# Rotary queries of a four-branch decoder kernel: turned with channels on partitions, stacked by way of DRAM

## The chip, the core and the metric

The kernel runs on one core of one Trainium2 chip. A core has TensorE (matrix products, PE in the profile, with its weight loads as PEld), VectorE (DVE), ScalarE (ACT), GpSimd (POOL) and SyncE (SP, which here issues every DMA). Matrix products land in PSUM, everything else works in SBUF, and large tensors lie in DRAM. The metric is the device time of one execution in microseconds (us), the median of several runs.

## The reference, cut to what matters

Two layers of a decoder trunk over 1024 tokens of width 1024. Each layer projects the stream, mixes the tokens in four ways (latent attention "MLA" with a rotary part, stick-breaking attention, forgetting attention "fox", attention to a memory), gates and projects each branch, merges them, and normalizes. The change touches only the rotary part of the MLA queries (four heads of 64 plain and 32 rotary channels):

```python
q = (_rms_norm(c_q, q_norm) @ w_qb).reshape(b, s, MLA_HEADS, MLA_NOPE + MLA_ROPE)
q_nope, q_pe = q[..., :MLA_NOPE], q[..., MLA_NOPE:]
q_pe = _rope(q_pe, cos[:, :, None, :], sin[:, :, None, :])
...
y_mla = _causal_softmax_attention(jnp.concatenate([q_nope, q_pe], -1),
                                  jnp.concatenate([k_nope, k_pe], -1), v_mla)
```

where `_rope` splits the 32 channels into halves x1, x2 and returns `[x1*cos - x2*sin, x1*sin + x2*cos]`. The angles depend on the token alone, so all heads and both layers share one table of 16 cosines and one of 16 sines for each token. The queries are scaled by 96 to the power -1/2.

## The kernel before, in words

**Arithmetic.** Every fp32 product is made of three fast products: an operand a is split into a high part (a rounded to the fast format fp32r) and a low part (what is left), and a.b is ah.bh + ah.bl + al.bh. `passes` (L242) emits these three matmuls for each 128-row block of the contraction (lines 245, 246, 247 of the profile). A split costs one copy and one subtraction. For the score products, the two parts of a head's 64 channels are stacked on 128 partitions (`stack_pair`, L286: ACT writes the high parts at L291, DVE the low parts at L295), so that one matmul contracts both.

**Buffers.** Most tiles of 128 x 512 words come from one pool "U" of 64 buffers; seven larger "W" buffers hold 128 x 1024. PSUM has eight banks: two of tag "pt" (`PT`), four of "pj" (`PJ`), two of "y". A tile that finds no free buffer waits for one to be released.

**Order.** The program is written as generators. A main one emits its instructions, and at each of its `yield`s a side one may emit a few of its own, so that TensorE has other work while a result is split. A scheduler then orders each engine's instructions once, at build time; on the chip each engine takes its own list in that order and waits at semaphores. DMAs are all in SP's list, so a DMA that has to wait holds those behind it.

**One layer.** Latent keys and values are projected and stored (`ckv_d`), then the fox branch runs in two pairs of heads: `run(units, filler, total)` emits the score and value products of the units and spreads `total` steps of a filler, here the projections of the next pair, over their gaps. The stick-breaking branch, the memory branch and the gates follow. Then comes the MLA preparation, which the change is about. Its main generator is, in order: `mla_ckvT` (latents with channels on partitions, rotary key), `mla_k`, `load_wq` (the query weights, split on POOL by `split_pool`, L153), `load_cq(1)`, `mla_v`, `split_cq(1)` (normalized query latents of tokens 512 to 1023, "half 1"), `load_cq(0)`, `mla_qpe(1)`, `split_cq(0)`, `mla_q(1)`, `mla_qpe(0)`, `mla_qpT(1)`, `mla_q(0)`, `mla_qpT(0)`. Beside it runs `early()`: the last gates, then 26 steps of the merge of a finished branch (products "pg" and "pb", accumulated by DVE into "acc" tiles). Each of the first 19 yields of the main generator, every fourth from the 20th, and some extra ones (a `yield n` stands for n steps) bring one such step; what is left is emitted when the main generator ends. The MLA units follow, heads 0 to 3, and in each head the query blocks in the order 3, 0, 2, 1 (256 tokens each): the first unit needs half 1, the second half 0.

**The rotary queries.** `mla_qpe(half)` (L990) projects the 4 x 32 rotary channels of 512 tokens with channels on partitions (nine matmuls into "qpeT"), copies them to SBUF on ACT (L994), yields three side steps, transposes the four 128 x 128 blocks back to tokens on partitions (L998), turns them there with six DVE operations of 128 x 256 (L703 to L708), scales them on POOL (L1004), and writes four tiles in which each head's 32 channels stand as high, low, high, low (four ACT copies at L1010, four DVE subtractions at L1011). `mla_qpT(half)` (L1015) transposes these for each head, four 128 x 128 blocks each (L1019), and ACT copies the result out of PSUM (L1021). The tile "qpe" of a head and half then holds 128 rows: the 32 channels as high, low, high, low. The score matmul at L369 contracts it with the rotary key.

Of the kernel before, what the change touches and what calls it, by code (L numbers as in the profile page):

```python
# [10 lines left out]
F32 = mybir.dt.float32  # L11
F32R = mybir.dt.float32r
I32 = mybir.dt.int32
AF = mybir.ActivationFunctionType
ALU = mybir.AluOpType
# [12 lines left out]
MG_FROM = 20  # L28
MG_EVERY = 4
CQ_STEPS = 1  # L30
QPE_STEPS = 3
MG_LATE = 16
Q_ORDER = (3, 0, 2, 1)
NB = S // P
# [31 lines left out]
def decoder_trunk(ctx: ExitStack, tc: tile.TileContext, x, x_t, mem_t, positions, w_a, w_s, mla_q_norm, mla_w_qb,  # L66
# [31 lines left out]
    def TMP(s="tmp"):  # L98
        return tp.tile([P, HALF], F32, tag="tmp", name=nm(s))
# [13 lines left out]
    def f(ap):  # L113
        return ap.bitcast(F32)
# [38 lines left out]
    def split_pool(src, h, l):  # L153
        i = pool.tensor_scalar(h, src, 1.0, 1.0, ALU.mult, ALU.mult)  # L154
        if hold[0] is not None:
            after(i, hold[0])
        pool.tensor_tensor(l, src, f(h), ALU.subtract)  # L157
# [27 lines left out]
    y_d = dp.tile([2 * KVR, S], F32, name="y_d")  # L185
    gt_d = dp.tile([KVR, S], F32, name="gt_d")
    c_d = dp.tile([4, S], F32, name="c_d")

    def rsqrt(dst, m, n):
        t = SM("rs_t", n)  # L190
# [138 lines left out]
    def pair_qkv(op, scale):  # L329
        op["q"], op["k"] = two_halves(), two_halves()  # L330
        yield from proj(stack_pair(op["q"], scale))
        yield from proj(stack_pair(op["k"], 1.0))
        vT = [None, None]

        def evac(ps, half):
            vT[half] = U("vT", F32)
            act.copy(vT[half], ps)
        yield from proj(evac)
        op["v"] = v_from_T(vT, NB)
        yield  # L340
# [149 lines left out]
    def chain(*gens):  # L490
        for g in gens:
            yield from g
# [30 lines left out]
    def run(units, filler, total, rest=True):  # L523


        order = list(units)
        gaps = sum(len(u.chunks()) * 2 + (1 if u.kind == "mem" else 2 + 2 * (u.qg // 2)) for u in units)
        done = [0, 0]

        def gap():  # L530
            done[0] += 1
            want = done[0] * total // gaps
            steps(filler, want - done[1])
            done[1] = want
# [12 lines left out]
        if rest:  # L547
            drain(filler)
# [60 lines left out]
    def angles():  # L609
# [7 lines left out]
        for dst, shift in ((sinT, 0.0), (cosT, 0.25)):  # L617
# [9 lines left out]
            dve.tensor_scalar(dst, dst, 3.1415925, -3.1415925, ALU.min, ALU.max)  # L627
            tfn(dst, dst, AF.Sin)

    for layer in range(DEPTH):  # L630
        last_layer = layer == DEPTH - 1
        xsrc = x[0] if layer == 0 else xs
# [68 lines left out]
        def rope(dst, src, cs, sn, t, mul):  # L701
            x1, x2 = src[..., 0:16], src[..., 16:32]
            mul(dst[..., 0:16], x1, cs, ALU.mult)  # L703
            mul(t, x2, sn, ALU.mult)
            mul(dst[..., 0:16], dst[..., 0:16], t, ALU.subtract)
            mul(dst[..., 16:32], x1, sn, ALU.mult)
            mul(t, x2, cs, ALU.mult)
            mul(dst[..., 16:32], dst[..., 16:32], t, ALU.add)  # L708
# [134 lines left out]
        drain(pair_qkv(fox[0], SC64))  # L843
        fox[0].update(new_op())
        ys[(2, 0)] = fox[0]["y"]
        run(fox_units(fox[0], 0), pair_qkv(fox[1], SC64), 49)
        fox[1].update(new_op())
        ys[(2, 1)] = fox[1]["y"]
        run(fox_units(fox[1], 1), pair_qkv(sb[0], SC64), 49)
# [93 lines left out]

        qpe = [[None, None] for _ in range(4)]
        cqT = [[], []]
        t4s = [[], []]
        cq_raw = [[], []]

        def load_cq(half):
# [21 lines left out]
        def load_wq():  # L971
            for k in range(3):
                raw = rp.tile([P, HALF], F32, tag="wr", name=nm("wr"))
                nc.sync.dma_start(raw[:, :384], mla_w_qb[layer, k * P:(k + 1) * P, :])
                h, l = U("wqh"), U("wql")
                sv = raw[:, :384].rearrange("p (h c) -> p h c", h=4)
                for c0, c1, d0 in ((0, 64, 0), (64, 96, 256)):
                    n = 4 * (c1 - c0)
                    hv, lv = (t[:, d0:d0 + n].rearrange("p (h c) -> p h c", h=4) for t in (h, l))
                    split_pool(sv[:, :, c0:c1], hv, lv)  # L980
                wq_h.append(h)
                wq_l.append(l)

        def mla_q(half):
            for pair in range(2):
                ps = PJ()
                yield from passes(ps, wsl(wq_h, wq_l, 3, pair * P), cqT[half], 3)
                stack_pair(ml[pair]["q"], SC96, True)(ps, half)

        def mla_qpe(half):  # L990
            ps = PJ("qpeT")
            yield from passes(ps, wsl(wq_h, wq_l, 3, 256), cqT[half], 3)
            qT = U("qT", F32)
            act.copy(qT, ps)  # L994
            yield QPE_STEPS
            ps = PT("qpe")
            for b in range(4):
                pe.transpose(ps[:, b * P:(b + 1) * P], qT[:, b * P:(b + 1) * P], ident)  # L998
            src = ps.rearrange("p (b h c) -> p b h c", b=4, h=4)
            qr = U("qr", F32).rearrange("p (b h c) -> p b h c", b=4, h=4)  # L1000
            qt = TMP("qt")[:, :256].rearrange("p (b h c) -> p b h c", b=4, h=4)
            cs, sn = (t[:, 4 * half:4 * half + 4].unsqueeze(2).broadcast_to((P, 4, 4, 16)) for t in (cosT, sinT))
            rope(qr, src, cs, sn, qt, dve.tensor_tensor)
            pool.tensor_scalar(qr, qr, SC96, 1.0, ALU.mult, ALU.mult)  # L1004
            for b2 in range(2):
                t4 = wp.tile([P, 2, 4, 4, ROPE], F32R, tag="W", name=nm("qt4"))
                for b in range(2):
                    t = t4[:, b]
                    qb_ = qr[:, 2 * b2 + b].unsqueeze(2).broadcast_to((P, 4, 2, ROPE))
                    act.copy(t[:, :, 0::2, :], qb_)  # L1010
                    dve.tensor_tensor(t[:, :, 1::2, :], qb_, f(t[:, :, 0::2, :]), ALU.subtract)  # L1011
                    t4s[half].append(t)
            yield

        def mla_qpT(half):  # L1015
            for h in range(4):
                pt = PT("qpT")
                for b in range(4):
                    pe.transpose(pt[:, b * P:(b + 1) * P].bitcast(F32R), t4s[half][b][:, h].rearrange("p a c -> p (a c)"), ident_r)  # L1019
                o = U("qpe")  # L1020
                act.copy(o, pt)  # L1021
                qpe[h][half] = o
                yield
            t4s[half].clear()


        yb = {}
# [79 lines left out]
        def step(f):  # L1107
            f()
            yield

        main = chain(mla_ckvT(), mla_k(0), mla_k(1), step(load_wq), step(lambda: load_cq(1)), mla_v(0), mla_v(1),
                     split_cq(1), step(lambda: load_cq(0)), mla_qpe(1), split_cq(0), mla_q(1), mla_qpe(0), mla_qpT(1), mla_q(0), mla_qpT(0))

        def early():
            for _ in side:
# [177 lines left out]
```

## Time and profile before

| | |
|---|---|
| median of 3 runs | 1590.06 us (1589.10 to 1591.06) |
| the profiled execution | 1590.93 us, span 1589.2 us from its first to its last instruction |
| mean granted TensorE clock in it | 0.995 |
| MLA preparation, layer 0 | about 470 to 528 us of the span |
| the same, layer 1 | about 1262 to 1320 us |

The profile shows one execution. Its page gives each engine's busy time, the chain of work that ended last, and groups of instructions by source line with count, total and mean time. Other views of the trace list the instructions of a stretch in order of time, the waits by who waited for whom, or the busy time of each engine in chosen stretches. In the list by time a row has start, duration (of a group, the time that it covers), engine, line, operation, output and inputs, count, and in brackets the idle time before it with what ended it. Matmuls overlap, so a matmul's duration is longer than its share of TensorE: that share is the distance from its start to the next one's.

### The profile page before, as it was taken

What the parts mean: (1) busy time and instruction counts of PE and PEld (TensorE: products, weight loads), DVE (VectorE), ACT (ScalarE), POOL (GpSimd) and SP (SyncE); (2) the same over time, 40 slices, a digit from 0 to 9 for tenths busy, and PEclk for the clock granted to TensorE, in tenths of its full rate; (3) what the DMA queues carried; (4) which work ended last, traced back from release to release, by engine and by line L of the source; (5) the groups of instructions that cost most, each with busy time, mean ns of one, the idle gap of its engine ahead of it and who ended that gap; (6) DMA issues with size and microseconds to landing.
All of it is one profiled execution on the core that took longest, in us unless ns stands there. A gap on an engine that the chain in (4) does not pass through costs nothing.

```text
span 1589.2 us, 24849 instructions
## 1 busy us (share of the span) xinstructions
PE 1559.1 (98%) x8454; PEld 1332.1 (84%) x8454; DVE 1035.0 (65%) x2025; ACT 739.9 (47%) x1632; POOL 834.8 (53%) x991
## 2 busy tenths in 40 slices
PE   9999999999999999999999999999999999999997
PEld 8888888888888888888788888888888878888885
DVE  7456689844436788872763566898444367888638
ACT  4355656534424656440423556555344346564302
POOL 5676435765544344671836655267655433446515
PEclk9999999999999999999999999999999999999999
DMA  6311112142233211252312221122422332212413
GB/s 183 114 57 55 48 39 64 54 127 61 79 102 110 68 58 40 82 177 73 116 61 87 60 61 44 37 64 64 116 61 84 100 104 70 64 49 75 146 53 113
DMA packets 86062, 127.93 MB, mean 80 GB/s; under 512 B 13424, under 2 KB 38832, under 8 KB 85936
## 3 DMA queue, kind: packets, MB, share of 16 engines
q1 hardware_dynamic: 85936, 126.34, 25.6%
q8 instruction: 67, 1.10, 0.3%
q14 instruction: 59, 0.48, 0.1%
HBM read 89.57 MB, written 19.96 MB: 69 GB/s over the span
## 4 chain that ended last, share of the span: by engine, by line
PE 85%; DVE 7%; issue 2%; DMA 2%; POOL 2%; ACT 1%; SPq 0%; DVEq 0%; ACTq 0%; POOLq 0%
PE pj L245 12%; PE pj L246 12%; PE pj L247 12%; PE y L485 7%; PE pt L455 6%; PE sc L366 3%; PE sc L367 3%; PE pb L245 3%; PE po L245 3%; PE po L247 3%; PE po L246 3%; PE pb L247 3%; PE pb L246 3%; PE pg L245 2%; PE pg L247 1%
## 5 line engine op out<-in xcount | busy, mean ns | idle before, releaser
L245 PE MATMUL pj<-xTh,wh 128*128 128x512 f32 x832 | 331.6, 399 | 2.2 <-DVE mx L424 1.4
L247 PE MATMUL pj<-xTh,wl 128*128 128x512 f32 x832 | 326.5, 392 | 0.0
L246 PE MATMUL pj<-xTl,wh 128*128 128x512 f32 x832 | 326.0, 392 | 0.0
L157 POOL TENSOR_TENSOR wl<-wr,wh 128x512 fp32r<-128x512 f32 x168 | 229.9, 1370 | 9.8
L154 POOL TENSOR_SCALAR wh<-wr 128x512 fp32r<-128x512 f32 x168 | 116.3, 692 | 209.7 <-PE pj L246 112.9
L146 DVE TENSOR_TENSOR pl<-pt,ph 128x384 fp32r<-128x384 f32 (+1 forms) x272 | 170.4, 638 | 75.3 <-ACT ph L145 73.4
L145 ACT CAST ph<-pt 128x384 fp32r<-128x384 f32 (+1 forms) x272 | 147.0, 550 | 133.9 <-PE pt L455 127.6
L247 PEld LDWEIGHTS pj<-xTh,wl 128*128 128x128 f32 x832 | 156.4, 188 | 31.8
L245 PEld LDWEIGHTS pj<-xTh,wh 128*128 128x128 f32 x832 | 156.8, 188 | 28.8 <-DVE mx L424 1.8
L246 PEld LDWEIGHTS pj<-xTl,wh 128*128 128x128 f32 x832 | 156.8, 189 | 25.4
L436 POOL TENSOR_SCALAR p<-p,sm 128x896 f32<-128x896 f32 (+7 forms) x128 | 102.4, 801 | 144.0 <-DVE sm L435 142.4
L125 ACT ACTIVATE p<-p,mx 128x896 f32<-128x896 f32 (+7 forms) x128 | 99.5, 778 | 70.7 <-DVE mx L424 63.2
L485 PE MATMUL y<-pl,v 128*128 128x256 f32 (+1 forms) x544 | 125.5, 307 | 0.0
L125 ACT ACTIVATE mg<-pg 128x512 f32<-128x512 f32 x128 | 76.4, 597 | 88.0 <-PE pg L247 58.9
L485 PE MATMUL y<-ph,v 128*128 128x256 f32 (+1 forms) x544 | 112.6, 284 | 0.1
L455 PE MATMUL pt<-ident_r,p 128*128 128x128 f32 x704 | 110.5, 272 | 0.0
L245 PE MATMUL pb<-ybh,wh 128*128 128x512 f32 x256 | 102.9, 402 | 2.2 <-DVE opB L295 1.0
L485 PEld LDWEIGHTS y<-ph,v 128*128 128x128 f32 x544 | 93.7, 190 | 12.3 <-issue 0.9
L429 DVE TENSOR_TENSOR_SCAN kt<-kt,unseen 128x896 f32<-128x896 f32 (+3 forms) x64 | 94.5, 1489 | 10.1 <-ACT kt L125 9.8
L246 PE MATMUL pb<-ybl,wh 128*128 128x512 f32 x256 | 100.1, 391 | 0.0
L247 PE MATMUL pb<-ybh,wl 128*128 128x512 f32 x256 | 100.1, 391 | 0.0
L416 POOL TENSOR_SCALAR_AFFINE_SELECT bt<-bt 128x128 f32<-128x128 f32 x64 | 47.5, 745 | 95.0 <-ACT bt L125 91.2
(277 smaller groups left out, 3658.0 us busy)
## 6 DMA issues: line engine op xcount, KB each, us to landing
wr<-in_w_s_dram SPq DMA_DIRECT2D x168, 256.0 KB, 2.6
s<-opA SPq DMA_DIRECT2D x128, 64.0 KB, 2.0
s<-opB SPq DMA_DIRECT2D x128, 64.0 KB, 2.0
wr<-in_w_out_dram SPq DMA_DIRECT2D x32, 256.0 KB, 2.6
xr<-in_x_t_dram SPq DMA_DIRECT2D x16, 256.0 KB, 5.1
ckb<-c_d SPq DMA_DIRECT2D x8, 512.0 KB, 3.8
y_d<-y SPq DMA_DIRECT2D x16, 256.0 KB, 2.0
y<-y_d SPq DMA_DIRECT2D x16, 256.0 KB, 3.6
```

The costliest lines, as they stand in the source:

```text
L125: i = act.activation(*args, **kw)
L145: act.copy(h, src)
L146: return dve.tensor_tensor(l, src, f(h), ALU.subtract)
L154: i = pool.tensor_scalar(h, src, 1.0, 1.0, ALU.mult, ALU.mult)
L157: pool.tensor_tensor(l, src, f(h), ALU.subtract)
L245: pe.matmul(ps, ah, bh, start=k == 0, stop=False)
L246: pe.matmul(ps, ah, bl, start=False, stop=False)
L247: pe.matmul(ps, al, bh, start=False, stop=k == nk - 1)
L429: dve.tensor_tensor_scan(kt[:, ::-1], kt[:, ::-1], unseen[:, S - w:][:, ::-1], 1.0, ALU.mult, ALU.max)
L436: pool.tensor_scalar(p, p, sm, 1.0, ALU.mult, ALU.mult)
L455: pe.transpose(pt[:, c:c + P], self.p[i][:, b * P:(b + 1) * P], ident)
L485: pe.matmul(u.y[:, q0 * P:256], u.op["v"][b][:, u.head, :], src[:, s * 256 + q0 * P:s * 256 + 256], start=j == 0 and n == 0, stop=j == n_c ...
```

## The change

The rotary part of the queries is turned where the projection leaves it, with channels on partitions and tokens along the row, and is brought to its stacked form by DMA.

- The rotary columns of the query weight are put down as first halves of all heads, then second halves (`load_wq`), so that rows 0 to 63 of the projection are the x1 and rows 64 to 127 the x2 of the four heads.
- Tables with channels on partitions are made once, in layer 0, as four extra steps of the filler of the first fox run (whose total goes from 49 to 53): for cosine and sine and each half, POOL spreads the table (tile "rows"), TensorE transposes four 128 x 128 blocks, ACT scales them (for the sine in two pieces, the second with a minus sign), and a DMA stores 256 KB to `tab_d`.
- `mla_qpe` reads the projection straight from PSUM, which is now a "pt" bank. Four DVE operations turn it, ACT rounds the high part, POOL subtracts for the low part, two DMAs store both to `qr_d`, and eight DMAs (two for each head) load 64 rows each: x1 and x2 of high and low, the same rows twice.
- `mla_qpT`, the transpositions in `mla_qpe`, the copies around them and the three side steps are gone. The main generator loads the tables beside the latents, and `mla_qpe(0)` now stands ahead of `mla_q(1)`.

```diff
@@ new, in layer 0 only
+    def rotary_tables():
+        for n, src in enumerate((cosT, sinT)):
+            for half in range(2):
+                rows = U("rows", F32)
+                pool.tensor_scalar(rows.rearrange("p (b r c) -> p b r c", b=4, r=8),
+                                   src[:, 4 * half:4 * half + 4, :].unsqueeze(2).broadcast_to((P, 4, 8, 16)), 1.0, 1.0, ALU.mult, ALU.mult)
+                ps = PT("tab")
+                for b in range(4):
+                    pe.transpose(ps[:, b * P:(b + 1) * P], rows[:, b * P:(b + 1) * P], ident)
+                t = TMP("tab")
+                if n == 0:
+                    act.activation(t, ps, AF.Copy, scale=SC96)
+                else:
+                    act.activation(t[0:64, :], ps[0:64, :], AF.Copy, scale=SC96)
+                    act.activation(t[64:128, :], ps[64:128, :], AF.Copy, scale=-SC96)
+                nc.sync.dma_start(tab_d[2 * half + n], t)
+                yield
@@
-        run(fox_units(fox[0], 0), pair_qkv(fox[1], SC64), 49)
+        tables = () if layer else rotary_tables()
+        run(fox_units(fox[0], 0), chain(pair_qkv(fox[1], SC64), tables), 49 if layer else 53)
@@ mla_qpe
-            ps = PJ("qpeT")
+            ps = PT("qpeT")
             yield from passes(ps, wsl(wq_h, wq_l, 3, 256), cqT[half], 3)
-            qT = U("qT", F32)
-            act.copy(qT, ps)
-            yield QPE_STEPS
-            ps = PT("qpe")
-            for b in range(4):
-                pe.transpose(ps[:, b * P:(b + 1) * P], qT[:, b * P:(b + 1) * P], ident)
...
-            rope(qr, src, cs, sn, qt, dve.tensor_tensor)
-            pool.tensor_scalar(qr, qr, SC96, 1.0, ALU.mult, ALU.mult)
-            for b2 in range(2):
...
-                    act.copy(t[:, :, 0::2, :], qb_)
-                    dve.tensor_tensor(t[:, :, 1::2, :], qb_, f(t[:, :, 0::2, :]), ALU.subtract)
+            cs, sn = tabs.pop(half)
+            r = U("qr", F32)
+            t = U("qt", F32)
+            dve.tensor_tensor(t[0:64, :], ps[64:128, :], sn[64:128, :], ALU.mult)
+            dve.tensor_tensor(t[64:128, :], ps[0:64, :], sn[0:64, :], ALU.mult)
+            dve.tensor_tensor(r, ps, cs, ALU.mult)
+            dve.tensor_tensor(r, r, t, ALU.add)
+            h, l = U("qrh"), U("qrl")
+            act.copy(h, r)
+            nc.sync.dma_start(f(qr_d[2 * half]), f(h))
+            pool.tensor_tensor(l, r, f(h), ALU.subtract)
+            nc.sync.dma_start(f(qr_d[2 * half + 1]), f(l))
             yield
+            src = f(qr_d[2 * half:2 * half + 2]).rearrange("a (t h c) n -> h (a t) c n", t=2, h=4)
+            for hd in range(4):
                 o = U("qpe")
+                for n in range(2):
+                    nc.sync.dma_start(f(o[64 * n:64 * n + 64, :]), src[hd])
+                qpe[hd][half] = o
+            yield
@@ mla_qpT, removed
-            for h in range(4):
-                pt = PT("qpT")
-                for b in range(4):
-                    pe.transpose(pt[:, b * P:(b + 1) * P].bitcast(F32R), t4s[half][b][:, h].rearrange("p a c -> p (a c)"), ident_r)
-                o = U("qpe")
-                act.copy(o, pt)
@@ the main generator
-        main = chain(mla_ckvT(), mla_k(0), mla_k(1), step(load_wq), step(lambda: load_cq(1)), mla_v(0), mla_v(1),
-                     split_cq(1), step(lambda: load_cq(0)), mla_qpe(1), split_cq(0), mla_q(1), mla_qpe(0), mla_qpT(1), mla_q(0), mla_qpT(0))
+        main = chain(mla_ckvT(), mla_k(0), mla_k(1), step(load_wq), step(lambda: load_cq(1)), step(lambda: load_tabs(1)), mla_v(0), mla_v(1),
+                     split_cq(1), step(lambda: load_cq(0)), step(lambda: load_tabs(0)), mla_qpe(1), split_cq(0), mla_qpe(0), mla_q(1), mla_q(0))
```

`load_tabs(half)` takes two U buffers and issues two loads of 256 KB from `tab_d`.

More of the change, by code (lines that the diff above doesn't have):

```diff
@@ L30 @@
 CQ_STEPS = 1
-QPE_STEPS = 3
 MG_LATE = 16
@@ L187, in decoder_trunk @@
     c_d = dp.tile([4, S], F32, name="c_d")
+    tab_d = dp.tile([4, P, HALF], F32, name="tab_d")
+    qr_d = dp.tile([4, P, HALF], F32R, name="qr_d")
     def rsqrt(dst, m, n):
@@ L945, in decoder_trunk @@
         cqT = [[], []]
-        t4s = [[], []]
         cq_raw = [[], []]
@@ L976, in load_wq @@
                 sv = raw[:, :384].rearrange("p (h c) -> p h c", h=4)
[L977 to L980, printed above, removed]
+                hv, lv = (t[:, :256].rearrange("p (h c) -> p h c", h=4) for t in (h, l))
+                split_pool(sv[:, :, 0:64], hv, lv)
+                hv, lv = (t[:, 256:384].rearrange("p (t h c) -> p t h c", t=2, h=4) for t in (h, l))
+                split_pool(sv[:, :, 64:96].rearrange("p h (t c) -> p t h c", t=2), hv, lv)
                 wq_h.append(h)
@@ L988, in mla_q, with load_tabs @@
                 stack_pair(ml[pair]["q"], SC96, True)(ps, half)
+        tabs = {}
+        def load_tabs(half):
+            tabs[half] = [U("tab", F32), U("tab", F32)]
+            for n, t in enumerate(tabs[half]):
+                nc.sync.dma_start(t, tab_d[2 * half + n])
         def mla_qpe(half):
-            ps = PJ("qpeT")
+            ps = PT("qpeT")
             yield from passes(ps, wsl(wq_h, wq_l, 3, 256), cqT[half], 3)
-            qT = U("qT", F32)
-            act.copy(qT, ps)
-            yield QPE_STEPS
@@ L996, in mla_qpe @@
-            ps = PT("qpe")
-            for b in range(4):
[L998 to L1002, printed above, removed]
-            rope(qr, src, cs, sn, qt, dve.tensor_tensor)
@@ L1004, in mla_qpe @@
-            pool.tensor_scalar(qr, qr, SC96, 1.0, ALU.mult, ALU.mult)
-            for b2 in range(2):
[L1006 to L1009, printed above, removed]
-                    act.copy(t[:, :, 0::2, :], qb_)
-                    dve.tensor_tensor(t[:, :, 1::2, :], qb_, f(t[:, :, 0::2, :]), ALU.subtract)
-                    t4s[half].append(t)
@@ L1013, in mla_qpe @@
-            yield
-        def mla_qpT(half):
-            for h in range(4):
-                pt = PT("qpT")
-                for b in range(4):
-                    pe.transpose(pt[:, b * P:(b + 1) * P].bitcast(F32R), t4s[half][b][:, h].rearrange("p a c -> p (a c)"), ident_r)
+            cs, sn = tabs.pop(half)
[3 more added lines that the diff above has]
+            dve.tensor_tensor(t[64:128, :], ps[0:64, :], sn[0:64, :], ALU.mult)
@@ L1022, in mla_qpT @@
-                qpe[h][half] = o
-                yield
-            t4s[half].clear()
+                for n in range(2):
+                    nc.sync.dma_start(f(o[64 * n:64 * n + 64, :]), src[hd])
+                qpe[hd][half] = o
+            yield
         yb = {}
```

## The prediction

> **What bounds the kernel now.** I read the page's first part first, then its chain.
>
> ```profile
> span 1589.2 us, 24849 instructions
> PE 1559.1 (98%) x8454; PEld 1332.1 (84%) x8454; DVE 1035.0 (65%) x2025; ACT 739.9 (47%) x1632; POOL 834.8 (53%) x991
> PE 85%; DVE 7%; issue 2%; DMA 2%; POOL 2%; ACT 1%; SPq 0%; DVEq 0%; ACTq 0%; POOLq 0%
> ```
>
> TensorE is busy for 98% of the span and is 85% of the chain that ended last. An average says nothing about one stage, so next the busy time by stretch, for the stretches that the change touches: the fox run of layer 0 that gets the tables, and the MLA preparation of both layers. The columns are PE, PEld, DVE, ACT, POOL, clock, DMA share and GB/s.
>
> ```profile
> 110.00:140.00 30.00, 30.00 (x170) 25.81 (x169) 14.97 (x48) 14.49 (x34) 16.54 (x25) 1.00 0.16 49
> 470.00:504.00 34.00, 32.59 (x170) 26.95 (x169) 18.14 (x31) 16.31 (x32) 15.72 (x22) 1.00 0.36 116
> 504.00:535.00 31.00, 30.21 (x157) 24.30 (x156) 22.67 (x47) 17.75 (x36) 5.05 (x6) 1.00 0.11 31
> 1296.00:1327.00 31.00, 30.22 (x157) 24.30 (x156) 23.07 (x47) 18.08 (x36) 5.05 (x6) 1.00 0.12 33
> ```
>
> TensorE is without a gap where the tables come in, and idle for 0.79 of 31 us where the transpositions go out. Both layers run the latter stretch alike, so one is worked out and doubled. The clock is full, and DMA has room. A transposition taken out of such a stretch is worth the TensorE time that it occupies.
>
> **Removed from TensorE.** The list by time, layer 0:
>
> ```profile
> 504.63 0.60 PE L998 MATMUL qpe<-ident_r,qT 128*128 128x128 f32 x4
> 505.07 0.60 PE L959 MATMUL rqb<-ident_r,rq 128*128 128x128 f32 x4
> 512.69 0.39 PE L245 MATMUL qpeT<-cqh,wqh 128*128 128x512 f32 x1
> 512.92 0.39 PE L246 MATMUL qpeT<-cql,wqh 128*128 128x512 f32 x1
> 524.76 0.46 PE L1019 MATMUL qpT<-ident_r,qt 128*128 128x128 f32 x4
> 525.06 0.47 PE L246 MATMUL pj<-cql,wqh 128*128 128x512 f32 x1
> 525.37 0.46 PE L1019 MATMUL qpT<-ident_r,qt 128*128 128x128 f32 x4
> 531.86 0.40 PE L247 MATMUL pg<-mrh,wl 128*128 128x512 f32 x1
> 532.81 0.36 PE L1019 MATMUL qpT<-ident_r,qt 128*128 128x128 f32 x2 [0.56 <-ACT qpe L1021]
> ```
>
> From start to start a 512-column matmul takes 512.92 - 512.69 = 0.23. A group of four L1019 transpositions takes 525.06 - 524.76 = 0.30, and the matmul behind it 525.37 - 525.06 = 0.31 in place of 0.23, so 0.38 for a group; eight groups a layer (two halves, four heads) make 3.0 us. A group at L998 takes 505.07 - 504.63 = 0.44; two make 0.9. Last, 531.86 + 0.23 = 532.09, and the next matmul starts at 532.81: 0.7 us in which PE waits for the ACT copy of an earlier transposed head. That wait goes with L1021; what is late next there is nothing that I see, since only score and merge products follow. Together 4.6 us a layer, 9.2 for both.
>
> Here the Trainium skill reads otherwise: "TensorE: Matmul & The Clock Gate", Part 4, gives about 275 ns for a 128x128 transposition in a kernel. By it, 80 removed and 16 added make 64 x 0.275 = 17.6 us, an estimate of mine from that figure. It is the duration of a single one; four of them start within 0.30 to 0.44 above, so I do not use it in the sum.
>
> **Added to TensorE.** Sixteen transpositions for the tables, once. The nearest row is the same operation in the same fox run:
>
> ```profile
> 122.36 0.60 PE L319 MATMUL vtp<-ident_r,vT 128*128 128x128 f32 x4
> 122.72 0.48 PE L366 MATMUL sc<-opA,opA 128*128 128x512 f32 x1
> 123.04 0.39 PE L367 MATMUL sc<-opA,s 128*128 128x512 f32 x1
> ```
>
> 0.36 for the group, and 0.32 in place of 0.23 behind it: 0.45, four times 1.8 us. No idle time covers it. ACT and POOL have half of that stretch free for the spreading and scaling, and the four stores end hundreds of microseconds before the first load.
>
> **Other engines.** In a half, ten DVE operations of 256 columns, nine ACT copies of 256 or 512 columns and a POOL scaling become four DVE operations, one ACT copy and one POOL subtraction. All of it lies beside TensorE (DVE is busy for 22.67 of 31 us there), so I cost the saving at nothing, and it can only help. The weight split keeps four POOL instructions a block with the same sizes: nothing. The three side steps that each `mla_qpe` gave away are not lost: by my count of yields, 42 side steps are all emitted inside the main generator before, 36 after, and the other six between `mla_q(0)` and the first scores. That moves work, and costs none. `mla_qpe(0)` stands directly behind `split_cq(0)`, whose splits it needs; `mla_q(1)`, emitted after it, is ready earlier, and the scheduler can put its 18 matmuls (4.1 us) into that gap.
>
> **The new round trip.** The rows for its steps: two DVE operations, the rounding copy, the POOL subtraction, DMA issue on SP, and DMA time to landing of a 256 KB store and load and a 64 KB move; then when the inputs are there and when the result is wanted.
>
> ```profile
> L961 DVE TENSOR_TENSOR cq<-cq,rqb x12: 677/681/687, 484.9 to 1299.1; 128x512 f32<-128x512 f32 x12
> L295 DVE SCALAR_TENSOR_TENSOR opB<-pj,opB x56: 692/694/694, 41.9 to 1325.7; 64x512 fp32r<-64x512 f32 x56
> L1021 ACT CAST qpe<-qpT x16: 585/588/618, 519.9 to 1326.7; 128x512 fp32r<-128x512 f32 x16
> L157 POOL TENSOR_TENSOR wl<-wr,wh x168: 1272/1292/2868, 21.7 to 1477.0; 128x512 fp32r<-128x512 f32 x168
> L346 SPq DMA_DIRECT2D s<-opA x64: 461/462/603, 47.0 to 1377.2; - x64
> L347 SPq DMA_DIRECT2D s<-opA x64: 461/588/718, 45.8 to 1377.7; - x64
> s<-opA SPq DMA_DIRECT2D x128, 64.0 KB, 2.0
> y_d<-y SPq DMA_DIRECT2D x16, 256.0 KB, 2.0
> y<-y_d SPq DMA_DIRECT2D x16, 256.0 KB, 3.6
> 502.78 0.59 ACT L994 COPY qT<-qpeT 128x512 f32<-128x512 f32 x1 [1.17 <-PE qpeT L247]
> 509.99 1.41 DVE L149 SCALAR_TENSOR_TENSOR cql<-cq,gq,cqh 128x512 fp32r<-128x512 f32 x2
> 528.03 0.40 PE L366 MATMUL sc<-opA,opA 128*128 128x512 f32 x1
> 534.49 0.27 PE L369 MATMUL sc<-kpe,qpe 128*128 128x128 f32 x1
> ```
>
> Four DVE operations take 2.7 us (two of 64 rows at 0.69, two of 128 at 0.68), the copy 0.6, the subtraction 1.3, the store 2.0. A load of 128 KB shows in no row; it lies between 2.0 and 3.6, and I take 2.8, the middle. Two issues come first, about 0.5 each. The first head is there 2.7 + 0.6 + 1.3 + 2.0 + 1.0 + 2.8 = 10.4 us after the projection (9.6 to 11.2), the fourth 3.2 us later.
>
> Half 1: the projection is ready at 502.78, so its first head lands near 513; the first scores start at 528.03, earlier by the transpositions that go, near 526. Cover 13 us. Half 0: the last low parts end at 509.99 + 1.41 = 511.40, nine matmuls of 0.23 follow, ready at 513.5, landed at 523.9, or 525.3 with two DVE operations of the merge ahead of it. It is wanted by the second unit at 534.49 - 4.6 = 529.9. Cover 4.6 to 6 us. So the round trip costs nothing as long as SP issues these DMAs when they are ready; later heads are wanted a unit run later.
>
> **The sum.** 1590.93 (the profiled execution: the span and 1.7 us around it) - 9.2 + 1.8 = 1583.5. New small waits where the order of a tight stretch is changed I bound by none and by the wait just removed, 0.7 a layer, and take the middle: 0.8 in all, so 1584.3. The profiled execution is 0.87 above the median of the runs, 1590.06; the median after should be 1583.5.
>
> **Rivals.**
>
> *Buffers.* Counting U tiles in the order of the program, I find at most 64 alive in the MLA preparation before, of 64, and 67 after, when `mla_q(1)` is stacked: the loaded tiles of half 0 come ahead of the release of the six latents of half 1. Then something waits for nine matmuls, 2.1 us a layer: 1583.5 + 4.2 = 1587.7, hardly to be told from no change. Against it: the loads take their tiles late, when those latents are likely gone.
>
> *SP's queue (slower).* One DMA that waits holds those behind it, and SP does wait for weight buffers:
>
> ```profile
> SPq L221 <- POOL wl L157: 409.8, 114, 15.5
> 513.08 0.47 SPq L346 DMA_DIRECT2D s<-opA  x1
> 520.98 0.33 SPq L221 DMA_DIRECT2D wr<-in_w_s_dram  x1
> ```
>
> The second and third row lie in the very stretch: after the swap of the first unit SP issues nothing for 520.98 - 513.55 = 7.4 us, until a weight buffer is free. Half 0's low part is ready to store near 513.5 + 4.6 = 518.1; behind that weight load it would wait 2.9 us, which the cover of 4.6 still takes. And the eight loads wait at the head for the store to land, with the next unit's swaps behind them. The price starts beyond 4.6 us of hold-up, the gain is used up at 4.6 + 6.6 / 2 = 7.9, and it is slower by 0.2% (3.2 us) from 9.5. At 13 us, between that and the longest hold-up of 15.5, it costs 2 x (13 - 4.6) = 16.8: 1600.3. Against it: in 504 to 535 SP issues only a handful of DMAs, and the scheduler lists a DMA where its own model has it ready.
>
> *More gain.* The projection moves from a "pj" bank to a "pt" bank, four large W tiles come free, and the order has more slack. The idle time of both stretches is 1.41 + 0.79 a layer; 0.56 of it is in the sum already (the bracket at 532.81). If the rest went too: 2 x 1.64 = 3.3 less, and none of the 0.8: 1579.4.
>
> *Transpositions at their full duration.* If each one held TensorE for the 0.27 us that the page counts for it, rather than the 0.07 to 0.11 between starts, 64 fewer would save 17.3:
>
> ```profile
> L455 PE MATMUL pt<-ident_r,p 128*128 128x128 f32 x704 | 110.5, 272 | 0.0
> ```
>
> That gives 1572.8, near what the skill's page above would make. The start times speak against it.
>
> **How the numbers follow.** A measurement of this kernel can tell about 0.2%, 3.2 us. Forecast 0.54, more gain 0.14, full duration 0.02: faster 0.70. Buffers 0.17: within 0.2%. SP's queue 0.13: slower. The range from 1578.5 to 1590.5 takes in forecast, more gain and buffers with about 1 us beyond their ends, and leaves out the other two, 0.15, and a little of the tails.
>
> **What would show it.** Right: no L998 or L1019 group in the MLA preparation; the first scores some 2 us earlier in layer 0 after allowing for the tables' 1.8, and the first half-0 scores 4.6; no wait of PE for the loaded "qpe" tiles; PE busy shorter by about 7. Wrong: PE or its weight load waiting on a DMA at L369; an SP issue gap ahead of the `qr_d` stores of over 5 us; PE waiting for DVE "opA" or "opB" in `mla_q(1)`, which would be the buffers; new idle time in the fox run beyond the tables' own.

## The result: slower by 1.2%

| | before | after |
|---|---|---|
| median | 1589.76 us (1589.10 to 1591.06) | 1610.79 us (1607.61 to 1611.93) |
| ratio | | 1.0124, interval 1.0112 to 1.0137 |
| the profiled execution | 1590.93 us, span 1589.2 | 1611.15 us, span 1609.4 |

The forecast was 1583.5 us. The changed kernel's page: the span, the engines' busy times, the shares of the chain that ended last.

```profile
span 1609.4 us, 24792 instructions
...
PE 1557.7 (97%) x8390; PEld 1328.4 (83%) x8390; DVE 1039.6 (65%) x2001; ACT 729.8 (45%) x1606; POOL 834.6 (52%) x995
...
PE 83%; DVE 7%; DMA 4%; issue 3%; POOL 2%; ACT 2%; SPq 0%; DVEq 0%; POOLq 0%; ACTq 0%
```

There are 64 transpositions fewer (8390 matmuls for 8454: 80 taken out, 16 put in for the tables). Yet PE is busy for only 1.4 us less, and its idle time, the span less the busy time, grew from 30.1 to 51.7 us. DMA rose from 2% to 4% of the chain. Both are too much for a change that leaves work out, so the next view is the same stretches as before (PE, PEld, DVE, ACT, POOL, clock, DMA share, GB/s), and the one behind them.

```profile
110.00:140.00 30.00, 30.00 (x168) 25.68 (x167) 13.24 (x40) 13.53 (x31) 18.30 (x29) 1.00 0.22 68
470.00:504.00 34.00, 31.79 (x169) 26.47 (x168) 19.07 (x33) 15.29 (x30) 15.45 (x22) 1.00 0.45 146
504.00:535.00 31.00, 23.81 (x86) 17.97 (x85) 17.20 (x24) 9.99 (x17) 4.47 (x4) 0.89 0.27 95
...
1296.00:1327.00 31.00, 25.43 (x102) 19.32 (x101) 17.86 (x26) 9.36 (x16) 6.38 (x6) 0.94 0.36 129
```

The fox run that makes the tables has no gap. The loss sits in the MLA preparation, in both layers: from 504 to 535 PE runs 86 matmuls where it ran 157, is idle for 7.2 us instead of 0.8, and its granted clock falls to 0.89. The first gaps and the first scores in PE's list by time:

```profile
510.42 0.49 PE L246 MATMUL qpeT<-cqh,wqh 128*128 128x512 f32 x1 [1.02 <-ACT cqh L147]
...
511.70 0.50 PE L247 MATMUL qpeT<-cql,wqh 128*128 128x512 f32 x1 [0.78 <-DVE cql L148]
...
520.74 0.50 PE L246 MATMUL pg<-mrh,wh 128*128 128x512 f32 x1 [1.49 <-DVE acc L1087]
...
523.49 0.76 PE L246 MATMUL pj<-cqh,wqh 128*128 128x512 f32 x1 [1.79 <-DVE opB L296]
...
529.47 0.50 PE L246 MATMUL pb<-ybh,wh 128*128 128x512 f32 x1 [2.11 <-ACT mg L124]
...
538.72 0.39 PE L367 MATMUL sc<-opA,opA 128*128 128x512 f32 x1
...
542.08 0.50 PE L368 MATMUL sc<-opA,s 128*128 128x512 f32 x1 [2.97 <-DMA s<-opA]
```

Six gaps, 10.16 us in layer 0, and the first scores come at 538.72 instead of 528.03. The last gap is no wait for a rotary tile: it is the swap of the first unit's plain channels (`s<-opA`), a transfer that the change does not touch. (Lines of after: 246 to 248 are the passes, 367, 368 and 370 the scores, 292 and 296 `stack_pair` on ACT and DVE, 147 and 148 the split of the latents, 1030 the copy "qrh", 1028 the last DVE operation of the turn, 1031 and 1033 the stores, 1039 the loads; experiments shift the last ones by one or two.)

Two lists say what held it. SP's DMAs, and then two steps of the chain of waits:

```profile
520.81 0.33 SPq L1031 DMA_DIRECT2D qr_d<-qrh  x1
522.18 0.32 SPq L1033 DMA_DIRECT2D qr_d<-qrl  x1
528.40 4.54 SPq L1039 DMA_DIRECT2D qpe<-qr_d  x8
533.04 0.52 SPq L348 DMA_DIRECT2D s<-opA  x1
533.68 0.51 SPq L347 DMA_DIRECT2D s<-opA  x1
```

```profile
522.18 6.08 DMA qr_d<-qrl
...
533.68 8.36 DMA s<-opA
```

A 256 KB store that was to take 2.0 us takes 6.08, and a 64 KB swap that took 2.0 takes 8.36. The store was issued 4.2 us after the last of eight loads of `qr_d`, the swap 0.7 us after the last of the next eight. What the DMA engines did meanwhile, by stretches of 3 us (the last three columns are the clock, the DMA share and GB/s):

```profile
516.00:519.00 3.00, 3.00 (x15) 2.35 (x13) 1.71 (x3) 0.00 (x0) 0.00 (x0) 1.00 0.26 98
...
525.00:528.00 3.00, 2.36 (x7) 1.54 (x5) 0.00 (x0) 0.34 (x1) 0.00 (x0) 0.69 0.24 79
...
531.00:534.00 3.00, 3.00 (x9) 2.31 (x9) 2.54 (x4) 0.87 (x2) 0.00 (x0) 0.55 0.26 100
```

The share is a quarter, and it stays there: as if 4 of 16 engines moved everything. At 100 GB/s eight loads of 128 KB (1.05 MB) need 10.5 us, so both were issued while loads were still moving. My reading is that what is issued behind them waits its turn on those four. The ACT list of the same stretch shows the second thing, that one copy holds up others:

```profile
509.13 0.62 ACT L1030 CAST qrh<-qr 128x512 fp32r<-128x512 f32 x1 [3.62 <-DVE qr L1028]
...
520.17 0.62 ACT L1030 CAST qrh<-qr 128x512 fp32r<-128x512 f32 x1 [6.87 <-DVE qr L1028]
520.70 0.59 ACT L292 ACTIVATE opA<-pj 64x512 fp32r<-64x512 f32 x1
...
527.65 0.59 ACT L292 ACTIVATE opB<-pj 64x512 fp32r<-64x512 f32 x1 [4.88 <-DMA qr_d<-qrh]
```

ACT stands idle for 6.87 us at the second "qrh", which needs the turn on DVE, and "opA" of `mla_q(1)`, whose product is done, is listed behind it. The last row adds a third suspect: an "opB" that waits for a store of "qrh", by which I read that it waits for the buffer being stored.

### The profile page after: what moved, and what is told of

Same layout as the page of the kernel before. It is cut to its first block, busy times and chain, and to the rows that moved or that the text cites. A ratio compares the mean times of both kernels' runs of the same rounds, so it can differ in the third digit from the quotient of the medians.

```text
span 1609.4 us, 24792 instructions
## 1 busy us (share of the span) xinstructions
PE 1557.7 (97%) x8390; PEld 1328.4 (83%) x8390; DVE 1039.6 (65%) x2001; ACT 729.8 (45%) x1606; POOL 834.6 (52%) x995
## 4 chain that ended last, share of the span: by engine, by line
PE 83%; DVE 7%; DMA 4%; issue 3%; POOL 2%; ACT 2%; SPq 0%; DVEq 0%; POOLq 0%; ACTq 0%
PE pj L246 12%; PE pj L248 12%; PE pj L247 11%; PE y L486 7%; PE pt L456 6%; PE sc L368 3%; PE sc L367 3%; PE po L248 3%; PE po L246 3%; PE po L247 3%; PE pb L246 3%; PE pb L248 3%; PE pb L247 3%; PE pg L246 1%; PE pg L248 1%
## 5 line engine op out<-in xcount | busy, mean ns | idle before, releaser
L153 POOL TENSOR_SCALAR wh<-wr 128x512 fp32r<-128x512 f32 x168 | 112.9, 672 | 222.5 <-PE pj L247 112.8
```

## Experiments

The first theory: (1) the loads use four DMA engines, since a head's 64 rows lie in DRAM as four runs of 16 (x1 and x2, high and low), and clog them for the stores and swaps behind; (2) what else is lost comes from the order in ACT's and DVE's lists. The rivals: buffers (the prediction's 67 for 64), and SP's queue as such, which e1 leaves in the same order. All comparisons are with the kernel before on the same chip, medians 1590.0 to 1590.2.

**e1, the even row order.** The rows of `qr_d` are put in the order half, channel, head, so that one head's 64 rows lie four apart, evenly through high and low. Bytes, DMAs and their order on SP stay the same.

```diff
-  (t[:, 256:384].rearrange("p (t h c) -> p t h c", t=2, h=4) for t in (h, l))
+  (t[:, 256:384].rearrange("p (t c h) -> p t h c", t=2, h=4) for t in (h, l))
...
-  .rearrange("a (t h c) n -> h (a t) c n", t=2, h=4)
+  .rearrange("a (t c h) n -> h (a t c) n", t=2, h=4)
```

(The weight columns and the tables follow the same order.)

> The rotary rows are ordered half, channel, head in place of half, head, channel, so that the 64 rows of one head are evenly spaced in DRAM and a load is one run of 64 rows, not 4 x 16; bytes, number of DMAs and all else stay. Four-engine theory (the changed kernel's loads occupy 4 of the 16 DMA engines: DMA share 0.26 at 516 to 519 us, 0.24 at 525 to 528, and whatever follows on those engines lands late): the store of the low part lands about 2 us after its issue and not 6, the swap of the first unit no longer lands 8 us late, 1584 to 1592 us. Buffer theory (67 tiles for 64 buffers, so the stacked queries wait): the wait of ACT for a buffer stays, 1600 or more. Order theory (the rotary queries of half 0 ahead of the plain queries of half 1 leave TensorE without work): 1600 or more. The Trainium skill, DMA: Bandwidth & Descriptors, section Why a DMA increments its semaphore by 16 and not by 1, says that a DMA runs on the largest number of engines up to 16 that divides the slowest dimension of both sides, which is 4 for the old loads and 16 for these.

1595.78 us (1592.46 to 1597.25), ratio 1.0034 (1.0022 to 1.0045): 15 of the 21 us are gone. Its page, its DMA groups (the last number is the median time to landing) and two of its stretches:

```profile
span 1590.7 us, 24795 instructions
...
PE 1550.8 (97%) x8390; PEld 1324.7 (83%) x8390; DVE 1035.1 (65%) x2001; ACT 729.6 (46%) x1606; POOL 836.3 (53%) x999
```

```profile
qpe<-qr_d SPq DMA_DIRECT2D x32, 128.0 KB, 3.0
...
qr_d<-qrl SPq DMA_DIRECT2D x4, 256.0 KB, 2.0
```

```profile
516.00:519.00 3.00, 2.40 (x11) 1.66 (x9) 2.53 (x4) 0.00 (x0) 0.00 (x0) 1.00 0.58 184
525.00:528.00 3.00, 3.00 (x15) 2.48 (x14) 2.79 (x5) 1.84 (x4) 0.00 (x0) 1.00 0.65 198
```

The same loads now land in 3.0 us and the stores in 2.0, at twice the rate, and no wait of PE for a DMA is left, though the swaps still stand behind the eight loads in SP's list. The time lies between the ranges written down, 1584 to 1592 for the four engines and 1600 or more for the others: the loads were the larger part, and not all. That leaves some 12 us over the forecast, with PE's gaps for "cqh", "cql", "acc" and "opB" as they were.

**e11, eight runs of eight.** To see whether it is the number of runs, the rows of a head are split once more; all else is as in the changed kernel.

```diff
-  .rearrange("a (t h c) n -> h (a t) c n", t=2, h=4)
+  .rearrange("a (k h c) n -> h (a k) c n", k=4, h=4)
```

> The changed kernel with the rows of a head in eight runs of eight instead of four runs of sixteen; order, copies and bytes are as in the changed kernel. Theory (a load uses as many engines as its source has runs): the DMA share while the loads move is 0.5 instead of 0.25, at about 195 GB/s; eight loads of 128 KB then take 5.4 us, no longer than SP needs to issue them (4.7), so the stores and swaps are hardly held: 1594 to 1600. Rival (any source that is not one even run of 64 is slow, by its descriptors): 0.25 again and 1608 to 1612.

1597.37 us (1595.77 to 1599.12), ratio 1.0046 (1.0030 to 1.0061). The same stretch of its trace:

```profile
516.00:519.00 3.00, 3.00 (x15) 2.46 (x14) 0.39 (x1) 0.00 (x0) 0.00 (x0) 1.00 0.47 162
```

0.47 for 0.26: close to half of the engines. Four runs, eight runs, one even run of 64: 1610.8, 1597.4, 1595.8. The step from four to eight is clear. The ranges of e11 and e1 overlap, and PE is idle for as long in both (40.1 and 39.9 us): eight engines were enough here, about when the loads move as fast as SP issues them (1.05 MB at 162 GB/s is 6.5 us, its eight issues took 5.2). The Trainium skill states the rule, on the page "DMA: Bandwidth & Descriptors", section "Why a DMA increments its semaphore by 16 and not by 1": a DMA uses the largest number of engines up to 16 that divides the slowest dimension of both its sides, and from SP it takes the lowest-numbered ones. The trace agrees with the first half: a slowest dimension of 4, 8 and 64, which makes 4, 8 and 16 engines by the rule, gave shares of 0.26, 0.47 and up to 0.65. The second half would say why swaps on all engines must queue behind loads on four; no run here shows which engines were used.

**e2, the buffers alone.** The tables, the turn and its two parts go to the larger W buffers; the loads stay as in the change.

```diff
-            h, l = U("qrh"), U("qrl")
+            hl = wp.tile([P, 2, HALF], F32R, tag="W", name=nm("qrhl"))
+            h, l = hl[:, 0], hl[:, 1]
```

(and the same for the tables and for "qr" and "qt")

> The tables, the turned queries and their high and low parts lie in W buffers in place of U buffers, which takes two to six tiles off the short pool at the critical place; the loads keep their shape. Four-engine theory: the loads of half 1 still hold up the stores of half 0 and the swaps; the 4.9 us wait of ACT for a buffer goes, but the first scores still wait for a swap: 1600 to 1609. Buffer theory: 1583 to 1592. Order theory: 1605 or more.

1611.48 us (1610.35 to 1612.40), ratio 1.0139 (1.0122 to 1.0156): no gain, and above the 1600 to 1609 of the theory as well. ACT's wait for a buffer is gone, and PE's wait for the swaps grew, `PE sc L368 <- DMA s<-opA`, 14.8 us for 7.7. The second eight loads go out at 526.71 instead of 528.40, but PE comes to its scores 5 us earlier and waits for a late swap there.

**e3, the order alone.** `mla_q(1)` ahead of `mla_qpe(0)`, loads as in the change.

```diff
-  mla_qpe(1), split_cq(0), mla_qpe(0), mla_q(1), mla_q(0))
+  mla_qpe(1), split_cq(0), mla_q(1), mla_qpe(0), mla_q(0))
```

> Only the main generator's order is set back: the plain queries of half 1 ahead of the rotary queries of half 0. Order theory: most of the loss goes, 1583 to 1594. Four-engine theory: the loads keep their four engines, and those of half 0 start later still, so 1602 to 1614. Buffer theory: six latents are released before half 0's tiles are taken, so 1585 to 1597.

1609.34 us (1608.37 to 1610.22), ratio 1.0123 (1.0108 to 1.0139). The gaps for "acc" and "opB" go, and the wait for the swaps grows to 19.3 us: again no gain clear of the noise while the loads clog.

**e4, no DRAM.** No stores and loads of `qr_d`; four ACT copies a half fill "qpe" with the rows of all heads as they lie, so this kernel leaves out the rotary part of the scores.

```diff
-                for n in range(2):
-                    nc.sync.dma_start(f(o[64 * n:64 * n + 64, :]), src[hd])
+                act.copy(o, r if hd % 2 else f(h))
```

> The round trip through DRAM is left out: no stores and no loads of the rotary queries; each head's tile is an ACT copy of the unstacked high part or of the turned queries (so the rotary part of the scores is not computed). Eight ACT copies a layer take the place of twenty DMAs. This measures what the transpositions taken off TensorE are worth, by the prediction's sum 7.4 us less the waits: 1581 to 1586 if only the DMAs cost the time (four-engine theory). Buffer and order theories: the orders and the tiles are those of the changed kernel, so 1595 or more.

1608.02 us (1607.29 to 1609.43), ratio 1.0116 (1.0101 to 1.0131): a plain miss, and worth its run. Without the round trip's DMAs it is as slow as the change. Its ACT list and its waits of PE (total, times, longest):

```profile
508.14 0.62 ACT L1030 CAST qrh<-qr 128x512 fp32r<-128x512 f32 x1 [3.63 <-DVE qr L1028]
...
510.88 1.95 ACT L147 ACTIVATE cqh<-cq,gq 128x512 fp32r<-128x512 f32 x3
...
522.50 0.62 ACT L1030 CAST qrh<-qr 128x512 fp32r<-128x512 f32 x1 [8.84 <-DVE qr L1028]
...
525.24 0.59 ACT L292 ACTIVATE opA<-pj 64x512 fp32r<-64x512 f32 x1
```

```profile
PE pj L246 <- DVE opB L296: 9.3, 4, 4.0
PE qpeT L246 <- ACT cqh L147: 6.5, 2, 3.2
```

The four copies stand behind "qrh" and ahead of "cqh" and "opA": 2.1 and 2.1 us of ACT work in the wrong place took two gaps on PE from 1.0 and 1.8 to 3.2 and 4.0. The run thus put a new cost where it took one out, and does not price the DMAs. So a part of the loss in the change may come from ACT's list too, and the next two take e1 as their base.

**e6, even rows and the order of e3.**

> The even row order with mla_q(1) again ahead of mla_qpe(0). Theory (lists): opA and opB of half 1 no longer stand behind the second qrh, so PE's waits for acc and opB, 1.49 and 1.79 a layer with the even row order alone, go; the wait for cqh and cql, 1.03 and 0.78, stays, since the first qrh still stands ahead of them: 1595.8 - 6.6 = 1589, between 1587 and 1591. Rival (tables and the missing cover cost the rest, not the order): within 2 of 1595.8.

1587.01 us (1584.95 to 1587.86), ratio 0.9981 (0.9972 to 0.9990): the same edit that gave nothing with the clogged loads is now worth 8.8. Its page and its ACT list:

```profile
span 1585.2 us, 24784 instructions
...
PE 1550.5 (98%) x8390; PEld 1323.8 (84%) x8390; DVE 1036.6 (65%) x2001; ACT 729.9 (46%) x1606; POOL 836.2 (53%) x999
```

```profile
510.81 0.58 ACT L292 ACTIVATE opA<-pj 64x512 fp32r<-64x512 f32 x1
...
520.06 0.62 ACT L1031 CAST qrh<-qr 128x512 fp32r<-128x512 f32 x1 [1.49 <-DVE qr L1029]
```

"opA" runs at 510.81 instead of 520.70, and ACT is idle for 1.49 ahead of the second "qrh" instead of 6.87.

**e7, even rows and "qrh" on DVE.**

```diff
-            act.copy(h, r)
+            dve.tensor_scalar(h, r, 1.0, 1.0, ALU.mult, ALU.mult)
```

> The even row order with the rounding copy qrh on DVE, right behind the addition that it needs, instead of on ACT. Theory (ACT's list): cqh and opA no longer wait behind a copy that waits for DVE; of the 5.1 us of gaps a layer the 1.03 before cqh goes and most of the 1.79 before opB, against two DVE operations of 0.4 to 0.7 more: 1590, between 1588 and 1593. Rival (DVE's list holds as much, since the turn itself stands ahead of cql, opA and acc there): 1595.8, or up to 2 more for the added DVE work.

1590.21 us (1589.23 to 1592.42), ratio 1.0002 (0.9993 to 1.0011): 5.6 less than e1. On DVE the copy stands right behind the operation that it waits for, so no ready work is held by that wait. The gap for "cqh" goes, the one for "opB" falls from 1.79 to 0.57, and the one for "acc", which now stands behind the copy, rises from 1.49 to 1.95.

**e9, both.**

> The even row order, mla_q(1) ahead of mla_qpe(0), and the copy qrh on DVE. Theory (lists): the order left 0.72 before cql and 0.84 before a merge product a layer, both behind a qrh on ACT; a DVE copy of 0.4 to 0.7 takes part of that back: 1587.0 less 2 x 0.8 = 1585.4, between 1583.5 and 1587. Rival (DVE's list becomes the holder, its cql stands behind the copy): 1587 to 1589.

1584.95 us (1583.23 to 1585.53), ratio 0.9967 (0.9954 to 0.9979): within 2 us of the forecast for the change.

**e5 and e10, the buffers again**, now on top of e1 and of e9.

> The even row order together with the seven tiles in larger buffers. Theory (the rest of the loss is the order in ACT's and DVE's lists): no wait of PE ends at a tile that had to find a buffer, so nothing moves: 1595.8 as with the even row order alone, between 1594 and 1597.5. Rival (buffers: with the loads out of the way the count of 67 for 64 shows): the two cqh copies that wait for a store of qr_d, about 1.4 a layer, come free: 1593 or less.

> The one before and also the seven tiles in larger buffers. Theory (no buffer is waited for once the order is eased): as the one before, within 1. Rival (buffers hold cqh and cql at the stores of qr_d, about 1.4 a layer on ACT): 2 to 3 less than it.

1592.69 us (1591.89 to 1595.53), ratio 1.0020 (1.0011 to 1.0029), beside the 1595.78 of e1, and 1582.66 us (1582.08 to 1585.54), ratio 0.9959 (0.9946 to 0.9971), beside the 1584.95 of e9. Both medians came out where the rival had put them (1593 or less; 2 to 3 less) and outside what the theory allowed, by 2 to 3 us. The ranges overlap, and the traces give less: PE is idle for 37.7 us in e5 and 39.9 in e1, but for 31.6 in e10 and 31.5 in e9. So the buffers cost up to 3 us while the other faults are there; what they cost beyond that stays open. e10 is the fastest kernel here. Its page:

```profile
span 1580.4 us, 24785 instructions
...
PE 1548.8 (98%) x8390; PEld 1323.2 (84%) x8390; DVE 1036.1 (66%) x2005; ACT 727.5 (46%) x1602; POOL 837.3 (53%) x999
```

**e13, `split_cq(0)` and `mla_q(1)` moved.** The order `split_cq(0), mla_qpe(1), mla_q(1), mla_qpe(0), mla_q(0)`, even rows, "qrh" on ACT.

> The even row order, split_cq(0) emitted ahead of mla_qpe(1) and mla_q(1) ahead of mla_qpe(0), all copies on ACT. Theory (lists): cqh of half 0 now stands ahead of the first qrh in ACT's list, so the 0.72 before cql goes too: 1587.0 less 1.5 = 1585.5, between 1583 and 1587, level with the forecast for the change within 2. Rival (the split then waits for the latents' load, which stands on SP behind weight loads): 1589 or more.

1586.92 us (1584.88 to 1588.52), ratio 0.9980 (0.9971 to 0.9988): at the upper edge, level with e6. "cqh" now runs ahead of the first "qrh" and its wait is gone, but another took its place:

```profile
518.28 0.47 PE L246 MATMUL pj<-cqh,wqh 128*128 128x512 f32 x1 [1.79 <-DVE opB L296]
```

On DVE the first three operations of the second turn (514.58 to 516.70) are now listed ahead of "opA" and "opB" of `mla_q(1)`. An order written by hand moves a wait as easily as it removes one.

**e8, the tables alone** in the kernel before.

> The kernel before with the rotary tables made and stored in the fox run, and nothing else of the change. The prediction has 1.8 us for them: 1591.8. Rival (hidden in slack that the run has): 1590, no difference. Rival (a filler of 53 steps shifts the run and costs more than its transpositions): 1593 or more.

1591.31 us (1587.82 to 1593.10), ratio 1.0005 (0.9996 to 1.0014): 0.8 more, between 0.6 less and 2.2 more. The predicted 1.8 fits, and so does nothing.

## Why the prediction was wrong

The sum can be closed with one subtraction, the span less PE's busy time.

| kernel | span | PE busy | PE idle | busy at half clock |
|---|---|---|---|---|
| before | 1589.2 | 1559.1 | 30.1 | 6.5 |
| after | 1609.4 | 1557.7 | 51.7 | 15.4 |
| e11, eight engines | 1596.2 | 1556.1 | 40.1 | 13.6 |
| e1, sixteen engines | 1590.7 | 1550.8 | 39.9 | 3.4 |
| e6, and the order | 1585.2 | 1550.5 | 34.7 | 0 |
| e9, and "qrh" on DVE | 1581.5 | 1550.0 | 31.5 | 3.4 |
| e10, and the buffers | 1580.4 | 1548.8 | 31.6 | 0 |

Each row is one execution; that of e1 is the fastest of its six, 3.3 us below their median. The last column is the part of PE's busy time that lies in stretches for which the trace has a granted clock of 0.5 (the last section shows two), without the one at the end of each execution.

The forecast in these terms: busy 1559.1 - 7.8 (the transpositions without the bracket of 0.7 a layer) + 1.8 = 1553.1, idle 30.1 - 1.4 + 0.8 = 29.5, span 1582.6. The changed kernel is 26.8 above it: 22.2 of idle and 4.6 of busy time. The idle part comes apart, in the order in which the faults were mended, as 11.8 for the loads, 8.4 for the lists and 2.0 that are left in e9; the busy part is nearly all clock.

- **The load, step "a load of 128 KB lies between 2.0 and 3.6": failed.** Sized by bytes from rows of other transfers, it was taken as 2.8. With even rows 3.0 was measured, so the size was right for another access pattern. The rows that were used said nothing about a source of four runs. With it failed "the round trip costs nothing as long as SP issues these DMAs when they are ready": SP did issue the stores when they were ready, and the low part's store then took 6.08 us and a swap behind the loads 8.36, where 2.0 was expected. The sum had no term for what a load does to the transfers behind it. From four engines to sixteen: 51.7 - 39.9 = 11.8 us of idle time.
- **"Other engines ... I cost the saving at nothing, and it can only help": failed.** Fewer instructions on ACT and DVE, but each turn is now one chain PE, DVE, ACT, POOL, and its one ACT copy stands in ACT's list ahead of work that was ready. By order and place of that copy: 39.9 - 31.5 = 8.4 us of idle time (5.2 by the order, 3.2 by the copy).
- **"The scheduler can put its 18 matmuls into that gap": failed.** It did put them there, but their results were not taken out: "opA" and "opB" waited behind "qrh" on ACT, and PE then waited for a "pj" bank (the gap of 1.79 that ends with "opB").
- **The round trip of 10.4 us with a cover of 4.6 to 6:** the cover was figured for the rotary tiles alone. No wait of PE for them is in the list of waits; it was the swap of the plain channels that came late. Half 0 also began late: its turn on DVE, put at 513.5, began at 517.24.
- **The clock had no term.** The same 8390 matmuls are 6.9 us longer in after than in e1 (1557.7 to 1550.8). At half clock a matmul starts 0.43 after the one before instead of 0.23, so 0.47 of such time is lost: by this estimate 0.47 x (15.4 - 3.4) = 5.6 of the 6.9, and 0.47 x (15.4 - 6.5) = 4.2 of the 4.6 above the forecast.
- **The transpositions, 9.2, and the tables, 1.8:** held. PE's busy time is 8.3 (e1) to 10.3 us (e10) below that of before, where -6.0 was worked out. With 0.47 of the last column taken off, again an estimate, before comes to 1556.0, after and e6 to 1550.5, e1 to 1549.2, e10 to 1548.8: 5.5 to 7.2 less. The tables alone (e8: 1559.0 busy, 3.4 of it at half clock, so 1557.4) come to 1.4 more, where 1.8 was worked out. "Full duration" (1572.8) is nowhere near. That e9 and e10 land at 1584.95 and 1582.66, around the 1583.5, is in part luck: both have less half-clock time than before, which the forecast did not count on.
- **Rivals.** The one on SP's queue (1600.3) came nearest: it named the loads that wait for the store, with the next swaps behind them, and that wait is there, but no weight load makes it, and in e1, with SP's list in the same order, PE no longer waits for a swap. Its mark for itself, a gap on SP ahead of the `qr_d` stores, is not there. Buffers: 3 us at most. The marks at L369 and in `mla_q(1)` half held: PE did wait on a DMA in the first unit, but at the swap, and on "opB" in `mla_q(1)`, but through ACT's list.

What is shown: that the row order of the loads costs, with a DMA share that follows it, by three row orders, and the hold by "qrh", by moving it in two ways. The busy times of e1 and e11, whose idle times are alike, differ by 5.3, and their half-clock time accounts for 0.47 x (13.6 - 3.4) = 4.8 of it. What is only argued: that the swap was late because it shares the four engines. The split of the 22.2 holds for this order of mending alone, since the order of the lists was worth nothing clear while the loads clogged.

## What to carry to other kernels

A DMA's duration belongs to its access pattern: before pricing one from another row, compare the slowest dimension of both sides, and ask what is issued next on the same engines. When work is taken off an engine, look in that engine's list for the instruction that now waits longest, and for what stands behind it that was ready. Two faults that cover each other must be mended together: the order alone gave 1.5 us, which is within the noise, and on top of the even rows 8.8.

## What the runs showed of the hardware

**Short gaps cost clock.** In the changed kernel, after gaps of 1.49 and 1.79 us within 4.2 us, matmuls start 0.43 us apart instead of 0.23 for some 3 us:

```profile
524.05 0.63 PE L247 MATMUL pj<-cql,wqh 128*128 128x512 f32 x1
524.48 0.63 PE L248 MATMUL pj<-cqh,wql 128*128 128x512 f32 x1
```

The same happens behind the gap of 2.11. In layer 0 of e1 the same gaps of 1.49 and 1.79 left the clock at 1.00. The trace holds the reason. The granted clock changes on a grid of 3.41 us: in after the stretches at half speed begin at 523.45, 530.28, 1311.93 and 1339.24, whole multiples of that apart. Cut on each run's own grid, first after, then e1 (PE's busy time stands behind the comma, the clock is the third number from the right):

```profile
520.04:523.45 3.41, 0.96 (x3) 0.49 (x3) 2.02 (x4) 2.29 (x4) 1.28 (x1) 1.00 0.55 194
523.45:526.87 3.42, 3.38 (x8) 2.74 (x9) 0.00 (x0) 0.00 (x0) 0.00 (x0) 0.50 0.31 97
526.87:530.28 3.41, 1.30 (x6) 0.74 (x6) 1.59 (x3) 2.48 (x5) 0.00 (x0) 1.00 0.11 31
530.28:533.69 3.41, 3.41 (x10) 2.67 (x9) 3.02 (x5) 1.56 (x3) 0.00 (x0) 0.50 0.25 95
```

```profile
517.48:520.89 3.41, 1.88 (x8) 0.90 (x6) 2.29 (x4) 1.54 (x3) 0.87 (x1) 1.00 0.50 118
520.89:524.30 3.41, 1.66 (x7) 1.42 (x8) 2.75 (x4) 2.28 (x5) 0.40 (x1) 1.00 0.37 144
```

In after PE is busy for 0.96 and 1.30 us of a window, and half speed follows each time. In e1 the grid cuts the same two gaps apart, PE is busy for 1.88 and 1.66, and the clock stays. So it is PE's idle share of one window that counts here, and not the length of a gap; where the limit lies is open, since in e5 half speed also follows a window, 792.04 to 795.45, in which PE is busy for 65%. The Trainium skill, "TensorE: Matmul & The Clock Gate", Part 1, has half speed follow at least one idle window of about 3.4 us, and the window running free. The free window and its length agree; but the windows that were followed by half speed here were not idle: PE was busy for 0.96 and 1.30 of their 3.41 us.

**A DVE addition of 0.69 us took 1.60** while a POOL subtraction ran; the second turn, with POOL idle, had 0.69. Layer 1 has the same pair, 1.61 and 0.69. From the lists of DVE and POOL of after:

```profile
507.49 1.60 DVE L1028 TENSOR_TENSOR qr<-qr,qt 128x512 f32<-128x512 f32 x1
...
519.39 0.69 DVE L1028 TENSOR_TENSOR qr<-qr,qt 128x512 f32<-128x512 f32 x1
```

```profile
507.26 1.29 POOL L156 TENSOR_TENSOR wl<-wr,wh 128x512 fp32r<-128x512 f32 x1
```

It starts inside the POOL operation and ends 0.54 after it, so about as long as if it had begun when POOL was done (508.55 + 0.69 = 509.24, measured 509.09). It lies on the chain that ends in the first "qrh".
